# A hybrid streaming encoder step: state-space preparation and first matrices moved into the first pass, bias copies into the state-space loop

## The chip, the cores and the metric

The kernel runs on one core of a Trainium2 chip. The metric is the device time of one execution in microseconds (us), the median of several runs. Engines are named as in the profile: PE (matrix engine), with PEld for its weight loads, DVE (vector), ACT (scalar), POOL (GpSimd) and SP (the queue that issues most DMAs).

## What is computed

One layer of a hybrid encoder, for 2048 prompt frames and 8 x 16 frames of running streams (17 tiles of 128 rows):

```python
h = _rms_norm(x, norm_gain)
z = jnp.einsum('bld,de->ble', h, w_in)
u, g_s, q, k, v, g_a = jnp.split(z, SPLITS, axis=-1)
y_s, hr, hi = _s5_branch(u, a_re, ..., h0_re, h0_im)
q = _rms_norm(heads(q), q_gain)
k = _rms_norm(heads(k), k_gain)
y_a = _band_attention(q, k, v, rel_table)
mixed = jnp.concatenate([y_s * jax.nn.silu(g_s), y_a * jax.nn.silu(g_a)], axis=-1)
y = x + jnp.einsum('ble,ed->bld', mixed, w_out)
```

`_s5_branch` is a state-space model: 32 groups of 16 channels, each driving a 64-dimensional complex diagonal state that is scanned along the frames, then a GELU and a GLU. The attention of the prompt sees its own 64-frame chunk and the 8 before it, with a learned bias over clipped distance; the running streams (`_cached_attention`) see 512 cached frames.

## The kernel before

**Foreground.** Each f32 product is three matmuls of split operands (`mm3`, L189 to L191: `whi`/`wlo` by `hhi`/`hlo`). One `mm3` is a *step* here; there are 1224. `inproj` makes three passes over the 17 tiles, with two groups of 512 columns each: `u` and `k`, then `v` and `q`, then `ga` and `gs`. A tile is 16 steps, a pass 272. Then come `glu` (8 steps a tile) and `outproj` (16). Weights arrive through five `wraw` buffers; `conv_w` splits a chunk (ACT `whi` L155, DVE `wlo` L156) and lets the next one load into the freed buffer. For the next pass 16 chunks are converted during the last tile of a pass (`due`). Things to be done some steps later are put off with `defer`: a `k` or `q` tile is scaled and squared on ACT, summed on DVE (`s` L279), raised to a power on POOL (L280, L281) two steps after its end, scaled on DVE (`zs` L284) at 8 steps, and transposed on PE (`pt` L294) at 14.

**Background.** A generator runs beside it: bias rows, S5, decode (the running streams), attention. It yields the cost of what it has emitted; each foreground step gives it a credit of 650 times a share, and when the credit is used up, the foreground goes on. So all engines' orders are fixed when the program is built. The share is `R_PREP` until the flag `u` is set (two steps after the first pass), `R_S5` until S5 has ended (flag `y`), `R_DEC` until decode has ended; in the attention it is computed so that it ends with step 1148. While weights are being converted the share is 0. A generator that yields `None` waits for a flag and gives its credit back.

**S5** (L449 to L949): first the preparation on DVE (exponentials, angles, powers, `X`, `Xs`, `AH0`); then it waits for `u`, since its later pool of tiles fits into memory only when the pool of the token tiles (`xt`) has been closed. After that come `build_a` to `build_e` (the matrices of a batch of 4 groups: DVE `CA`, `VBp`; PE `pv` and `pk`; ACT `VB`, `kr`; eight small DMAs into `T`), `tables` (rotation tables, six POOL operations a group), `load_u`, `perm_u` and `step_a` (U from memory, P on ACT, `ut` on PE, UT on ACT), and a loop over 8 batches with 6 slots each.

```python
        while not self.flags.get("u"):
            yield None
```

**Bias copies:** `bias_rows` (L955) writes the bias line and then 8 copies of it, each repeated 128 times, from POOL's queue to `tl_d` in DRAM (L965). Decode and attention read them.

Of the kernel before, what the change touches and what calls it, by code (L numbers as in the profile page):

```python
# [7 lines left out]
F32 = mybir.dt.float32  # L8
# [10 lines left out]
NG, CH, NS = 32, 16, 64  # L19
# [20 lines left out]
def ap_of(t, offset, pat):  # L40
    return bass.AP(tensor=t.tensor, offset=t.offset + offset, ap=pat)


class Build:
# [148 lines left out]
    def inproj(self):  # L193
        nc, I, tc = self.nc, self.I, self.tc
        wp, hp, ev = self.wp, self.hp, self.ev
        xst = ExitStack()
        xp = self.pool(xst, "xt")
        x3 = I["x"].rearrange("(t p) d -> t p d", p=128)
        passes, W = self.PASSES, self.W

# [1 line left out]
        XR = {}  # L202

        def load_tok(t):
            xt = xp.tile([128, 1024], F32, tag="xtok", name="xtok")
            nc.sync.dma_start(xt, x3[t])
            return xt

# [179 lines left out]
        for ps in range(3):  # L388
            for ti, t in enumerate(TILES):
                if ps == 0 and ti < 2:  # L390
                    continue
                last = ti == NT - 1
                if last:
                    self.due(self.step + 4, 1.25, 16 if ps < 2 else 8)
                for gi in range(2):
                    g = passes[ps][gi]
                    z = self.psm.tile([128, 512], F32, tag="mm", name="z")
                    for k in range(8):
                        self.busy = bool(self.cq)
                        self.mm3(z, hs[0][:, k], hs[1][:, k], W[ps, gi, k], k == 0, k == 7)  # L400
                        if gi == 0 and k == 1:
                            if ps == 2 and last:
                                while not self.flags.get("y"):
                                    yield 500
                                self.glu_load(TILES[0])
                            else:
                                nxt = conv_h(ps * NT + ti + 1)
                        self.tick()
                        if ps == 2 and last and gi == 1 and k == 3:
                            self.glu_tr(TILES[0])  # L410
                            self.glu_load(TILES[1])
                        yield 650
                    EV[g](g, t, z)
                hs = nxt
            if ps == 0:
                xst.close()
            if ps == 0:
                self.defer(2, lambda: self.flags.update(u=True))

# [29 lines left out]
    def s5(self):  # L449
# [188 lines left out]
        yield 500  # L638
        pst.close()

        while not self.flags.get("u"):
            yield None

        mp = self.pool(st, "s5m", side="right", bufs=2)
        Tm = []
# [216 lines left out]
            nc.sync.dma_start(y4[c0:c0 + n, :, b * GB * CH:(b + 1) * GB * CH], y[0:n])  # L862

        SL = self.SL_S5
        for n in range(3):
            load_u(0, n)
        build_a(0)
        for q in range(2):
            for _ in tables(q):
                yield 2 * SL  # L870
        perm_u(0, 0)
        build_b(0)
        yield SL
        for n in range(3):
            if n == 1:
                build_d(0)
            feed(n)
            if n == 0:
                build_c(0)
            if n == 2:  # L880
                build_e(0)
            yield SL
        for b in range(NBATCH):
            nx = b + 1 < NBATCH
            for sl in range(6):
                if 2 <= sl:
                    step_gs(b, sl - 2)
                if sl < 4:
                    step_b1(b, sl)
                    step_swap(b, sl)  # L890
                if 1 <= sl < 5:
                    step_rot(b, sl - 1)
                if b and 1 <= sl < 4:
                    step_y(b - 1, sl - 1)
                yield SL
                if 2 <= sl:
                    step_h(b, sl - 2)
                if sl == 5:
                    step_fin(b)
                q = b * GB + sl  # L900
                tg = tables(q + 2) if sl < 4 and q + 2 < NG else iter(())
                next(tg, None)
                if b and sl < 3:
                    step_c(b - 1, sl)
                if nx:
                    if sl == 0:
                        build_a(b + 1)
                    if sl == 3:
                        build_b(b + 1)
                        yield SL  # L910
                    if sl == 4:
                        build_c(b + 1)
                        yield SL
                        build_d(b + 1)
                        yield SL
                    if sl >= 3:
                        feed(3 * (b + 1) + sl - 3)
                    if sl == 5:
                        build_e(b + 1)
                yield SL  # L920
                for _ in tg:
                    pass
# [32 lines left out]
    def bias_rows(self):  # L955
# [5 lines left out]
        nc.gpsimd.dma_start(self.rl_d, rl)  # L961
        self.st_line.close()
        yield 600
        for h in range(NH):
            nc.gpsimd.dma_start(self.tl_d[h], ap_of(self.rl_d, 768 * h, [[0, 128], [1, 767]]))  # L965
            yield 1000


    def decode(self):
# [507 lines left out]
                    self.use_spare()  # L1477


    R_PREP, R_S5, R_DEC = 0.2, 0.48, 0.75  # L1480
    MARGIN = 0
    att_left = 136
    C_PREP = 400
# [123 lines left out]
```

## Time and profile before

| what | value |
|---|---|
| median of 3 runs | 1227.88 us (1225.18 to 1228.61) |
| the profiled execution | 1226.13 us |
| its span (first to last instruction) | 1224.3 us |
| PE busy | 1193.0 us (97%) |
| DVE / ACT / POOL busy | 742.6 / 597.7 / 366.6 us |
| granted PE clock, mean | 0.995 of 2.4 GHz |
| read / written | 169.48 / 67.80 MB |

The profile is of one execution. Busy time of PE is counted from modelled ends of pipelined matmuls, so a stretch with PE fully busy is one in which it never stood still. A wait is the idle time of an engine just before an instruction, with what ended it behind the arrow. The first pass runs from the start to about 205 us, the second to about 460, the third to about 704; S5's loop fills 250 to 575 us, decode 600 to 670, attention 705 to 1160.

### The profile page before, as it was taken

The page shows a single profiled execution, that of the slowest core. Times are in us where ns is not written, and L with a number is a line of the kernel's source. Part 1 is how long each engine was busy: PE and PEld are TensorE (multiplying, and loading weights), DVE is VectorE, ACT ScalarE, POOL GpSimd, SP SyncE. Part 2 cuts the span into 40 slices and gives each one's busy share as a digit, 9 for nine tenths or more (in the row PEclk, how much of TensorE's full clock was granted, in tenths as well). Part 3 has the DMA queues.
Part 4 walks back from the last instruction along what each step waited for, and adds up shares of the span by engine and source line. Part 5 has one row for each costly group of instructions (what it writes and reads, how often), then busy time and mean ns, then how long its engine had stood idle before and what let it go on. Part 6 is the DMA issues. An engine that isn't in the chain of part 4 may idle for free.

```text
span 1224.3 us, 18936 instructions
## 1 busy us (share of the span) xinstructions
PE 1193.0 (97%) x6687; PEld 983.1 (80%) x6687; DVE 742.6 (61%) x1391; ACT 597.7 (49%) x1159; POOL 366.6 (30%) x455
## 2 busy tenths in 40 slices
PE   8999999899999998999999999999999999999998
PEld 5788888777788876887777878788888888888876
DVE  5324556868999988985444456565565555555511
ACT  6434446266666656553232346565654555455410
POOL 2433242557767735540000011111211121121120
PEclk9999999999999998999999999999999999999999
DMA  8876556655545567433895688897877777767243
GB/s 252 262 250 181 155 177 202 195 142 129 149 123 151 135 195 214 110 93 88 270 382 171 204 247 245 255 265 205 217 221 215 206 240 241 196 205 225 73 136 107
DMA packets 190119, 236.58 MB, mean 193 GB/s; under 512 B 58136, under 2 KB 122656, under 8 KB 189000
## 3 DMA queue, kind: packets, MB, share of 16 engines
q1 hardware_dynamic: 189016, 232.15, 64.2%
q0 software_dynamic: 864, 3.21, 0.8%
q8 instruction: 53, 0.87, 0.3%
q14 instruction: 42, 0.34, 0.1%
q10 hardware_dynamic: 144, 0.00, 0.0%
HBM read 169.48 MB, written 67.80 MB: 194 GB/s over the span
## 4 chain that ended last, share of the span: by engine, by line
PE 78%; DMA 6%; DVE 6%; POOL 3%; ACT 3%; issue 2%; SPq 1%; DVEq 0%; ACTq 0%; POOLq 0%
PE z L189 19%; PE z L191 18%; PE z L190 18%; PE o L1218 6%; PE pt L1200 5%; PE s L1170 5%; DMA wraw<-in_w_in_dram 3%; PE pt L294 1%; PE o L1057 1%; PE y L843 1%; SPq L701 1%; PE y L842 1%; PE v L771 1%; ACT whi L155 1%; PE s L1015 1%
## 5 line engine op out<-in xcount | busy, mean ns | idle before, releaser
L189 PE MATMUL z<-whi,hhi 128*128 128x512 f32 x816 | 339.2, 416 | 1.4 <-ACT whi L155 0.7
L190 PE MATMUL z<-wlo,hhi 128*128 128x512 f32 x816 | 321.3, 394 | 3.3 <-DVE wlo L156 3.1
L191 PE MATMUL z<-whi,hlo 128*128 128x512 f32 x816 | 320.7, 393 | 0.5 <-DVE hlo L231 0.5
L189 PEld LDWEIGHTS z<-whi,hhi 128*128 128x128 f32 x816 | 154.1, 189 | 38.9 <-issue 5.1
L190 PEld LDWEIGHTS z<-wlo,hhi 128*128 128x128 f32 x816 | 154.5, 189 | 36.5 <-DVE wlo L156 8.0
L191 PEld LDWEIGHTS z<-whi,hlo 128*128 128x128 f32 x816 | 154.0, 189 | 34.3 <-DVE hlo L231 1.0
L1207 ACT ACTIVATE pth<-pt 128x640 fp32r<-128x640 f32 (+4 forms) x128 | 81.7, 639 | 129.3 <-PE pt L1200 89.4
L1208 DVE TENSOR_TENSOR ptl<-pt,pth 128x640 fp32r<-128x640 f32 (+4 forms) x128 | 94.6, 739 | 60.6 <-ACT pth L1207 59.7
L189 PE MATMUL z<-whi,mh 128*128 128x512 f32 x272 | 113.7, 418 | 0.0
L1115 POOL MEMSET bias<- 64x64 f32 x32 | 4.7, 146 | 363.5 <-DMA bias<-tl_d 250.0
L1189 ACT ACTIVATE sn<-sn,mn 128x640 f32<-128x640 f32 (+4 forms) x128 | 96.9, 757 | 29.5 <-DVE mn L1180 29.4
L191 PE MATMUL z<-whi,ml 128*128 128x512 f32 x272 | 107.1, 394 | 1.3 <-POOL ml L1415 1.3
L190 PE MATMUL z<-wlo,mh 128*128 128x512 f32 x272 | 106.7, 392 | 0.0
L1180 DVE CUSTOM_DVE_ANT_0 sn<-s,bias 128x640 f32<-128x640 f32 (+4 forms) x128 | 93.3, 729 | 11.4 <-PE s L1170 10.4
L1170 PE MATMUL s<-ks,q 128*128 128x320 f32 (+1 forms) x448 | 87.4, 311 | 0.0
L1200 PE MATMUL pt<-ident,sn 128*128 128x128 f32 x560 | 83.0, 274 | 3.9 <-DVE ptl L1208 3.1
L1170 PEld LDWEIGHTS s<-ks,q 128*128 128x128 f32 x448 | 74.7, 188 | 11.1 <-DVE mn L1180 1.2
L1200 PEld LDWEIGHTS pt<-ident,sn 128*128 128x128 f32 x560 | 64.9, 140 | 22.5 <-ACT sn L1189 10.0
L231 DVE TENSOR_TENSOR hlo<-xraw,hhi 128x1024 fp32r<-128x1024 f32 x49 | 60.9, 1242 | 20.7 <-ACT hhi L228 20.6
L280 POOL TENSOR_SCALAR s<-s 128x8 f32<-128x8 f32 x34 | 15.9, 468 | 182.9 <-DVE s L279 182.3
L1228 DVE TENSOR_TENSOR ot<-o,tmp 64x512 f32<-64x512 f32 x32 | 22.0, 689 | 74.5 <-ACT tmp L1226 74.5
L191 PEld LDWEIGHTS z<-whi,ml 128*128 128x128 f32 x272 | 51.0, 188 | 13.2 <-POOL ml L1415 1.7
(268 smaller groups left out, 2171.3 us busy)
## 6 DMA issues: line engine op xcount, KB each, us to landing
xraw<-in_xT_dram SPq DMA_DIRECT2D x49, 512.0 KB, 4.5
q<-qt_d SPq DMA_DIRECT2D x64, 256.0 KB, 8.6
ks<-kt_d SPq DMA_DIRECT2D x28, 512.0 KB, 5.6
vhl<-vp_d SPq DMA_DIRECT2D x28, 512.0 KB, 6.7
wraw<-in_w_in_dram SPq DMA_DIRECT2D x48, 256.0 KB, 4.5
bias<-tl_d SPq DMA_DIRECT2D x32, 320.0 KB, 6.3
mt<-mt_d SPq DMA_DIRECT2D x17, 512.0 KB, 7.4
x<-in_x_dram SPq DMA_DIRECT2D x34, 256.0 KB, 5.8
```

The costliest lines, as they stand in the source:

```text
L189: mm(z, a, whi, start=first, stop=False)
L190: mm(z, a, wlo, start=False, stop=False)
L191: mm(z, b, whi, start=False, stop=last)
L231: nc.vector.tensor_sub(lo, raw, fv(hi))
L1170: nc.tensor.matmul(ps_s[:, bank, 0:wp], Q[n, x2][:, s, 128 * a:128 * a + 128], KS[n][:, s, c0:c0 + wp], start=(x2 == 0), stop=(x2 == 1))
L1180: nc.vector.tensor_tensor_reduce(out=o, in0=i0, in1=i1, scale=1.0, scalar=3e38, op0=OP.add, op1=OP.min, accum_out=mn)
L1189: nc.scalar.activation(out=sn[:, 0:w], in_=sn[:, 0:w], func=AF.Exp, scale=-1.0, bias=mn, accum_out=SUM[n][:, a, s:s + 1])
L1200: nc.tensor.transpose(t[:, k], pr[:, 128 * k:128 * k + 128], self.ident)
L1207: nc.scalar.activation(out=h, in_=t[:, 0:w], func=AF.Copy)
L1208: post.append(lambda: nc.vector.tensor_tensor(out=l, in0=t[:, 0:w], in1=fv(h), op=OP.subtract))
L1218: nc.tensor.matmul(o[:, a0:a1], VB[n][:, j, s, :], t[:, 3 * a0 + j + a0:4 * (a1 - 1) + j + 1:4], start=(y == 0 and j == 4), stop=(y == 1 a ...
L1228: post.append(lambda: nc.vector.tensor_tensor(out=ot[mine], in0=o[mine], in1=tmp[mine], op=OP.add))
```

## The change

1. The pool `xt` is gone; the token tile lives in the slot `vhl`, which is free in the first pass.
2. The wait for `u` moves behind the preparation, `build_a` to `build_e` of batch 0, the tables of the first four groups and `build_a(1)`. So these stand in the first pass; only `load_u`, `perm_u` and `step_a` come behind the wait. Later tables start with group 4.
3. The eight bias copies move from `bias_rows` into the S5 loop, one a batch.
4. `R_PREP` goes from 0.2 to 0.27, `R_S5` from 0.48 to 0.42.

```diff
@@ inproj
-        xst = ExitStack()
-        xp = self.pool(xst, "xt")
...
-            xt = xp.tile([128, 1024], F32, tag="xtok", name="xtok")
+            xt = ev.tile([128, 1024], F32, tag="vhl", name="xtok", bufs=1)
...
-            if ps == 0:
-                xst.close()
@@ s5
         pst.close()
-        while not self.flags.get("u"):
-            yield None
...
         SL = self.SL_S5
+
+        build_a(0)
+        yield SL
+        for q in range(4):
+            for _ in tables(q):
+                yield SL
+        build_b(0)
+        yield SL
+        build_c(0)
+        yield SL
+        build_d(0)
+        yield SL
+        build_e(0)
+        yield 2 * SL
+        build_a(1)
+        while not self.flags.get("u"):
+            yield None
         for n in range(3):
             load_u(0, n)
-        build_a(0)
-        for q in range(2):
-            for _ in tables(q):
-                yield 2 * SL
+        yield 2 * SL
         perm_u(0, 0)
-        build_b(0)
         yield SL
         for n in range(3):
-            if n == 1:
-                build_d(0)
             feed(n)
-            if n == 0:
-                build_c(0)
-            if n == 2:
-                build_e(0)
             yield SL
         for b in range(NBATCH):
             nx = b + 1 < NBATCH
+            self.bias_copies(b)
...
-                tg = tables(q + 2) if sl < 4 and q + 2 < NG else iter(())
+                tg = tables(q + 2) if sl < 4 and 4 <= q + 2 < NG else iter(())
...
-                    if sl == 0:
+                    if sl == 0 and b:
                         build_a(b + 1)
@@ bias_rows
-        for h in range(NH):
-            nc.gpsimd.dma_start(self.tl_d[h], ap_of(self.rl_d, 768 * h, [[0, 128], [1, 767]]))
-            yield 1000
+
+    def bias_copies(self, h):
+        self.nc.gpsimd.dma_start(self.tl_d[h], ap_of(self.rl_d, 768 * h, [[0, 128], [1, 767]]))
@@ shares
-    R_PREP, R_S5, R_DEC = 0.2, 0.48, 0.75
+    R_PREP, R_S5, R_DEC = 0.27, 0.42, 0.75
```

Counted in the built orders by foreground steps: the preparation on DVE stands at steps 56 to 178 instead of 134 to 305; the first matmul of the loop (`v`) at 297 instead of 330; from one batch to the next are 44 steps instead of 38; the last `y` matmul of S5 at 676 instead of 664; decode's first product at 724 instead of 709, attention's at 832 instead of 820, its last at 1146 instead of 1145. The bias copies stand some 45 steps apart, the last near step 610; decode reads them at 701.

The order on PE, where the first batch's U enters the S5 work (`ut` transposes it, `pk` is the matrix of batch 0, both write one PSUM buffer). Before:

```order
L733 MATMUL ut<-ident,P 128x128 x4
L686 MATMUL pk<-CA,X 16x128 x4
L189 MATMUL z<-whi,hhi 128x512
L190 MATMUL z<-wlo,hhi 128x512
L191 MATMUL z<-whi,hlo 128x512
```

In the change (lines of the new file), with the foreground's `pt` of the last `k` tile of the first pass ahead of it:

```order
L292 MATMUL pt<-ident,zs 128x128 x4
L189 MATMUL z<-whi,hhi 128x512
L190 MATMUL z<-wlo,hhi 128x512
L191 MATMUL z<-whi,hlo 128x512
L189 MATMUL z<-whi,hhi 128x512
L190 MATMUL z<-wlo,hhi 128x512
L191 MATMUL z<-whi,hlo 128x512
L727 MATMUL ut<-ident,P 128x128 x4
```

`pk` of batch 0 no longer stands behind `ut`: it is now in the first pass, five steps behind `pv`. And `ut` stands 34 steps earlier, two steps behind the `pt` of the hand-over.

The order on ACT at that place, from the last weight conversions of the second pass. Before:

```order
L155 ACTIVATE whi<-wraw,gain 128x512 x5
L303 ACTIVATE kt<-pt,kg_88 128x4x128
L274 ACTIVATE sq<-z,rstd 128x512
L275 ACTIVATE zs<-z,rstd 128x512
L228 ACTIVATE hhi<-xraw 128x1024
```

In the change:

```order
L155 ACTIVATE whi<-wraw,gain 128x512 x5
L713 ACTIVATE P<-U 128x512
L301 ACTIVATE kt<-pt,kg_88 128x4x128
L713 ACTIVATE P<-U 128x512
L728 ACTIVATE UT<-ut 128x4x128
L272 ACTIVATE sq<-z,rstd 128x512
L273 ACTIVATE zs<-z,rstd 128x512
L226 ACTIVATE hhi<-xraw 128x1024
```

Two copies of U and one of `ut` now stand ahead of the foreground's `sq`, `zs` and `hhi`. On SP the first three U loads have moved likewise, from behind the next tile's `xraw` to between the fourth and the fifth of the last weight loads.

The order on POOL where the tables begin. Before, behind the wait for `u`:

```order
L648 MEMSET T_2120 128x512
L648 MEMSET T_2122 128x512
L756 TENSOR_TENSOR cos<-cb 128x256
L757 TENSOR_TENSOR ttmp<-sb 128x256
L758 TENSOR_TENSOR cos<-cos,ttmp 128x256
L761 TENSOR_TENSOR sin<-sb,cb 128x256
L762 TENSOR_TENSOR ttmp<-cb,sb 128x256
L763 TENSOR_TENSOR sin<-sin,ttmp 128x256
L280 TENSOR_SCALAR s_2176<-s_2176 128x8
L281 TENSOR_TENSOR s_2176<-s_2176,nhalf 128x8
```

In the change, at the same place of the foreground:

```order
L278 TENSOR_SCALAR s_2167<-s_2167 128x8
L279 TENSOR_TENSOR s_2167<-s_2167,nhalf 128x8
L968 DMA tl_d<-rl_d 128x767
L278 TENSOR_SCALAR s_2287<-s_2287 128x8
L279 TENSOR_TENSOR s_2287<-s_2287,nhalf 128x8
L750 TENSOR_TENSOR cos<-cb 128x256
L751 TENSOR_TENSOR ttmp<-sb 128x256
L752 TENSOR_TENSOR cos<-cos,ttmp 128x256
```

The memsets and the first four tables are gone from here; they stand in the first pass now, nine table operations in a row ahead of an `s` there. A bias copy has come in between two `s`.

## Rows read from the trace of the kernel before

**Rows 1.** The page, part 1: busy time, share of the span, instructions.

```profile
PE 1193.0 (97%) x6687; PEld 983.1 (80%) x6687; DVE 742.6 (61%) x1391; ACT 597.7 (49%) x1159; POOL 366.6 (30%) x455
```

**Rows 2.** Stretches: start:end length, busy by engine (instructions), PE clock, DMA share, GB/s.

```profile
36.00:200.00 164.00, 164.00 (x753) 135.60 (x753) 74.17 (x140) 73.94 (x111) 62.35 (x89) 1.00 0.65 195
200.00:225.00 25.00, 22.58 (x96) 17.99 (x95) 20.84 (x39) 14.20 (x21) 6.45 (x5) 0.93 0.84 282
225.00:320.00 95.00, 90.12 (x469) 72.03 (x468) 78.19 (x126) 51.17 (x108) 66.17 (x76) 1.00 0.51 137
320.00:445.00 125.00, 125.00 (x703) 101.94 (x702) 113.32 (x195) 77.58 (x175) 85.05 (x95) 1.00 0.55 144
445.00:485.00 40.00, 35.68 (x169) 27.42 (x169) 34.43 (x53) 24.95 (x46) 16.32 (x17) 0.91 0.73 217
...
705.00:860.00 155.00, 149.65 (x876) 127.07 (x876) 91.11 (x208) 89.61 (x204) 25.48 (x44) 1.00 0.83 245
```

**Rows 3.** PE's waits, 225 to 320 us: total us, times, longest.

```profile
PE pk L686 <- ACT UT L734: 2.0, 1, 2.0
PE pt L294 <- DVE zs L284: 1.5, 2, 1.0
PE ut L733 <- ACT VB L679: 1.3, 1, 1.3
```

**Rows 4.** PE's waits, 445 to 485 us.

```profile
PE pt L294 <- DVE zs L284: 2.8, 2, 2.4
```

**Rows 5.** PE in order of time: start, length, and in brackets the idle time before.

```profile
250.51 0.41 PE L686 MATMUL pk<-CA,X 128*16 128x128 f32 x8 [1.96 <-ACT UT L734]
```

**Rows 6.** POOL and PE in order of time, 232 to 245 us.

```profile
232.94 0.99 POOL L648 MEMSET T<- 128x512 f32 x2 [5.76 <-DVE AH0s L637]
...
239.21 1.77 POOL L763 TENSOR_TENSOR sin<-sin,ttmp 128x256 f32<-128x256 f32 x1
...
244.27 0.63 PE L294 MATMUL pt<-ident,zs 128*128 128x128 f32 x4 [1.02 <-DVE zs L284]
```

**Rows 7.** ACT, DVE and PE in order of time, 443 to 473 us.

```profile
446.39 2.55 ACT L155 ACTIVATE whi<-wraw,gain 128x512 fp32r<-128x512 f32 x4
...
457.16 2.79 ACT L155 ACTIVATE whi<-wraw,gain 128x512 fp32r<-128x512 f32 x4 [6.24 <-DMA wraw<-in_w_in_dram]
...
443.75 0.76 DVE L661 TENSOR_TENSOR CA<-CA,btmp 128x576 f32<-128x576 f32 x1
...
450.57 2.73 DVE L156 SCALAR_TENSOR_TENSOR wlo<-wraw,gain,whi 128x512 fp32r<-128x512 f32 x4
...
472.84 1.09 PE L294 MATMUL pt<-ident,zs 128*128 128x128 f32 x4 [2.35 <-DVE zs L284]
```

**Rows 8.** U and P: duration ns min/median/max, first and last start; landing of U's DMAs.

```profile
L711 SPq DMA_DIRECT2D U<-u_d x24: 538/590/1111, 232.9 to 496.7; - x24
L719 ACT ACTIVATE P<-U x24: 610/626/647, 245.6 to 523.8; 128x512 f32<-128x512 f32 x16, 16x512 f32<-16x512 f32 x8
...
DMA to landing us min/median/max: 3.3/4.1/5.2
```

**Rows 9.** SP's queue and PE in order of time at the first hand-over.

```profile
215.60 2.74 SPq L139 DMA_DIRECT2D wraw<-in_w_in_dram  x5
...
221.35 0.63 PE L191 MATMUL z<-whi,hlo 128*128 128x512 f32 x1
```

**Rows 10.** A stretch of that hand-over (columns as in rows 2).

```profile
218.00:220.00 2.00, 1.27 (x6) 1.18 (x7) 2.00 (x4) 0.49 (x1) 1.28 (x1) 0.79 1.03 383
```

**Rows 11.** POOL's groups, 225 to 560 us: busy us, mean ns of one, idle before.

```profile
L763 POOL TENSOR_TENSOR sin<-sin,ttmp 128x256 f32<-128x256 f32 x32 | 30.5, 953 | 2.5
...
L756 POOL TENSOR_TENSOR cos<-cb 128x256 f32<-128x256 f32 x32 | 24.1, 753 | 24.6 <-DVE t L809 24.6
```

**Rows 12.** The bias copies on POOL: issue in ns, first and last start; landing.

```profile
L965 POOL DMA_DIRECT2D tl_d<-rl_d x8: 523/626/662, 37.6 to 73.6; - x8
...
DMA to landing us min/median/max: 4.9/7.1/8.2
```

## Prediction, made before the changed kernel ran

> **What bounds the kernel now.** I read the page's busy times first: PE works 1193.0 of 1224.3 us [rows 1], so a change that adds and removes no matmul can only win or lose in the 31 us in which PE is idle and in the time it runs at its lower clock. The stretches say where that is [rows 2]: between 36 and 200 us PE is never idle, nor between 320 and 445; it is idle 95.00 - 90.12 = 4.9 us from 225 to 320, where the state-space (S5) work begins, and 40.00 - 35.68 = 4.3 us from 445 to 485, where the second pass hands over to the third. There the granted clock is 0.91 too: 0.09 x 40 = 3.6 us lost at the lower of the two levels (1.2 instead of 2.4 GHz), which it took after PE had stood still. DVE is then the busiest engine behind PE: 113.32 of 125.00 us from 320 to 445.
>
> PE's waits name the causes. From 225 to 320 [rows 3]: 2.0 us `pk` for ACT's `UT` copy, 1.5 us `pt` for DVE's `zs`, 1.3 us `ut` for ACT's `VB` copy. From 445 to 485 [rows 4]: 2.8 us `pt` for `zs`, 4.3 - 2.8 = 1.5 us in other waits. The reader should see that no wait of the first group is for data from far away: each is a short PE step that stands right behind another one whose result an engine in between has not yet copied, or (`zs`) a small POOL operation behind the rotation tables.
>
> **Part A, the start of the S5 work (225 to 320 us): -3.9 us.** The 2.0 us wait is one event: `pk` stands directly behind `ut` on PE, both use the one `ut` buffer, and PE waits 1.96 us until ACT has copied it [rows 5]. In the change that `pk` (batch 0) stands in the first pass with five foreground steps ahead of it, about 5 x 0.7 us, so all 2.0 us go. (A step is 0.7 us: 164 us [rows 2] hold 753 matmuls, 52 to a tile of 16 steps, so 0.71.) Of the `zs` wait 1.0 us is the tables: POOL clears two T tiles from 232.94, works on one table until 240.98, and only then comes to `s`; PE gets its `pt` at 244.27 after 1.02 us [rows 6]. The change puts these tables ahead of the wait for `u`; 1.0 us goes. What is left of the group, 1.9 us, is the ordinary traffic of the first batches, now spread over 44 steps a batch instead of 38; I let half of it go, 0.9. Sum 3.9; bounds 2.0 (the one event alone) and 4.9 (all).
>
> **Part B, second pass to third (445 to 485 us): -2.5 us.** ACT makes the first `whi` at 446.39 to about 447.1, but DVE, which has run without a gap through build_a and a rotation, makes the first `wlo` at 450.57 [rows 7]: 3.4 us of DVE queue. The next five weight chunks are only loaded when `wlo` frees their buffers, and ACT waits 6.24 us for them [rows 7]; the chain goes round three times and ends in `zs` and PE's longest wait, 2.35 us to 472.84 [rows 7]. The share R_S5 falls by 0.42/0.48 = 0.875, so DVE's share of 0.91 must fall to between 0.91 x 0.875 = 0.79 (all of it background) and 0.91 (none of it). I take half of the queue away, 1.7 us, and with it 0.8 of the 3.6 us of clock. Bounds: 0 (the loads set the chain whatever DVE does) and 4.3 + 3.6 = 7.9.
>
> **Part C, the new wait at the first hand-over (216 to 226 us): +1.0 us.** The first U loads move from 232.9 us [rows 8] to the moment `u` is set: on SP they now stand inside the last five weight loads, on ACT the first `P` copy stands ahead of `kt`, `sq` and `zs`, on PE the first `ut` stands two steps behind `pt`. Four of the five loads issued from 215.60 in 2.74 us [rows 9] bring the first U to 217.8; landing takes 3.3 to 5.2, median 4.1 [rows 8], and `P` 0.63: 222.5 us. PE would stand there after the matmul that starts at 221.35 [rows 9], 0.43 later: a wait of 0.7 us (0 to 1.8). I take 1.0, because the DMA engines are full at that time (1.03, 383 GB/s [rows 10]). ACT is late by some 3 us behind `P`; its `sq` and `zs` free a PSUM buffer that PE next needs eight steps later, over 5 us, so that costs nothing. Bound above: rival 2.
>
> **Part D, what is moved into the first pass: 0.** DVE's preparation moves from steps 134 to 305 to steps 56 to 178, between evictions. From 36 to 200 us DVE has 74.17 of 164 us, POOL 62.35 [rows 2], and PE does not wait; what now runs after about 218 us and before POOL is let go at 232.94 [rows 6], 15 us at most, and one more build_a (six operations like the one of 0.76 us in [rows 7]) come in: 20 us of DVE. POOL gets four tables of six operations, 0.75 to 0.95 us each [rows 11]: about 20 us. Bunched, it is tight: three operations (2.6 us) every 800/(0.27 x 650) = 4.6 steps or 3.2 us are 0.81 of POOL, and its present work is 0.38; for 37 steps (26 us) it falls behind by 0.19 x 26 = 5 us. The cover is that `s` is asked for two steps after a tile's end and `pt` stands at fourteen, 8.5 us later. If the tables took that cover, it would cost what the wait behind a table costs now, 1.0 us [rows 6], in each of the two tiles. The xtok tile in the `vhl` slot costs nothing: `v` writes there only in the second pass. The wait for `u` holds only generators back, no engine.
>
> **Part E, the bias copies: 0.** Eight issues of 0.63 us on POOL, 4.9 to 8.2 us to land [rows 12], go from 37.6 to 73.6 us into the S5 loop, one a batch. PE does not wait where they leave [rows 2]; POOL has 85.05 of 125 us where they come, plus about 2. Behind each stand the next `s` and table operations, 0.6 us later. The last is issued some 90 steps before decode reads it.
>
> **Part F, the later end: 0.** S5 ends 12 steps later, so attention starts at step 832 instead of 820 and is packed into 315 instead of 327 steps, 4% denser. PE's idle time in its first part, 155.00 - 149.65 = 5.4 us from 705 to 860 [rows 2], would grow by 0.2; at 25% growth 1.3 is the bound.
>
> **The sum:** -3.9 - 2.5 + 1.0 = -5.4 us. The profiled execution took 1226.1 us (span 1224.3), so it would be 1220.7; the median of the runs lies 1.8 above it, 1227.9, so I forecast 1222.5.
>
> **Rivals.** *1: the loads alone set the second hand-over.* Then B is 0 and the sum -2.9: 1225.0. For it: ACT's 6.24 us wait is for a DMA; against it: the loads start when `wlo` frees the buffers, and `wlo` was late.
>
> *2: the U wait takes the place of what A removes (slower).* One transfer in the wrong place: U's 256-byte pieces behind five weight loads. Priced by the slowest landing for a transfer of this kernel on a busy queue, 8.2 us [rows 12]: U at 226.0, `P` 226.6, a wait of 4.8 us instead of 1.0 right after the wait that already lowered the clock; the lower level held for one more such stretch (0.07 x 25 = 1.75 us lost from 200 to 225 [rows 2]) makes it 6.6. With A at its lower bound and B at 0: +4.6, 1232.5. It decides from the point where the U landing takes about 7 us. For it: PE, ACT and SP all carry the chain at one place; against it: no landing of U shown is over 5.2 us [rows 8].
>
> *3: the copies' issue blocks POOL.* The row shows 0.52 to 0.66 us an issue in the first pass [rows 12], where DVE is 0.45 busy; none is shown beside a DVE at 0.91. If each held POOL until a `zs` comes as late as the one behind the tables, 1.02 us of PE [rows 6], eight cost 8.2: 1230.7. Against it: `s` stands a table's length away from most copies. The Trainium skill, SBUF — State Buffer (SBUF: two separate sides), speaks against the change here: a DMA issued from GpSimd needs a port that DVE's two-port operations lock, and one that takes about 620 ns alone took about 3100 beside a copy. By its figure, an estimate, eight issues would hold POOL 8 x 2.5 = 20 us more; it also says that only copies and the like lock it so, and DVE in this loop runs two-input operations, so I give it little.
>
> *4: more goes than I let go:* A at 4.9 and B at 5: 1219.0. That the change doesn't do what it says (preparation not done when `u` is set) is excluded by the order: build_a(1), the last piece, stands on DVE ahead of the conversion of the second pass's weights.
>
> **Chances.** The forecast 0.50 (its own range 1219 to 1225), rival 1 0.22, rival 2 0.13, rival 3 0.07, rival 4 0.08. A measurement of this kernel can tell about 0.3%, 3.7 us, from no change: below 1224.2 is faster, above 1231.6 slower. Forecast and rival 4 give 0.54 faster (0.04 of the forecast lies within), rival 1 and half of rival 3 make 0.30 the same, rival 2 and the other half 0.16 slower. The range, 1217.0 to 1230.0, leaves out rival 2, half of rival 3 and the extreme of B.
>
> **What would show it.** Right: no `pk` wait for `UT` and no `pt` wait behind a table between 225 and 320 us; the first `wlo` of the second hand-over less than 2 us behind its `whi`; PE idle there under 3 us. C is right if PE's first `ut` waits for `P` by 0 to 1.8 us. Wrong: a `ut` wait of several us with the clock at 1.2 GHz behind it (rival 2); the second hand-over unchanged with DVE idle before `wlo` (rival 1); POOL issues of over 2 us (rival 3); PE idle between 36 and 200 us (D). If all four show as forecast and the time still doesn't fall, the loss must lie in the denser attention.

## The result: slower by 0.9%, with the profile after

| what | before | changed |
|---|---|---|
| median | 1228.25 us (6 runs) | 1236.91 us (6 runs, 1235.08 to 1244.26) |
| ratio of the runs | | 1.0087, 95% interval 1.0066 to 1.0107 |
| the profiled execution | 1226.13 us | 1235.08 us |
| its span | 1224.3 us | 1233.3 us |

Forecast were 1222.5 us and a range up to 1230.0. PE's work is the same (first line, against [rows 1]), so again only its idle time and its clock can differ. The page's busy times of the changed kernel:

```profile
PE 1194.2 (97%) x6687; PEld 983.8 (80%) x6687; DVE 735.7 (60%) x1391; ACT 598.9 (49%) x1159; POOL 365.4 (30%) x455
```

The stretches of the changed kernel, columns as in [rows 2]:

```profile
200.00:225.00 25.00, 22.36 (x101) 17.84 (x99) 18.62 (x24) 15.30 (x23) 7.57 (x6) 0.99 0.83 258
225.00:320.00 95.00, 92.20 (x477) 74.68 (x476) 67.19 (x119) 56.55 (x118) 49.65 (x56) 0.97 0.59 162
320.00:445.00 125.00, 124.78 (x694) 101.41 (x693) 111.23 (x183) 73.25 (x162) 86.43 (x98) 1.00 0.56 151
445.00:485.00 40.00, 35.96 (x188) 28.42 (x187) 33.49 (x49) 28.11 (x54) 16.74 (x18) 1.00 0.72 225
...
705.00:860.00 155.00, 144.68 (x823) 121.77 (x821) 83.40 (x197) 83.76 (x193) 26.86 (x45) 0.98 0.85 244
860.00:1140.00 280.00, 275.98 (x1621) 239.60 (x1620) 159.72 (x305) 146.76 (x271) 45.67 (x59) 1.00 0.72 215
```

From 225 to 320 us PE is idle 2.8 instead of 4.9 us, but at a granted clock of 0.97 instead of 1.00, which takes 0.03 x 95 = 2.9 us (from 200 to 225 us it is the other way round, 0.99 instead of 0.93). So little is won there, but the main loss is not where the change was made. The GLU's first product says so: up to it PE has the same 3811 instructions in both kernels, and the changed one is 1.3 us ahead (changed, then before):

```profile
703.77 0.39 PE L189 MATMUL z<-whi,yh 128*128 128x512 f32 x1
```

```profile
705.05 0.39 PE L189 MATMUL z<-whi,yh 128*128 128x512 f32 x1
```

From there to the end of PE's work it takes 525.4 us, the kernel before 514.4, with the same 2876 instructions. The loss stands from 705 us on: 10.3 instead of 5.4 us idle up to 860, where the clock falls too, and 4.0 us from 860 to 1140, where the kernel before has this row (1.4 us):

```profile
860.00:1140.00 280.00, 278.63 (x1636) 243.21 (x1634) 160.66 (x306) 147.57 (x272) 49.90 (x62) 1.00 0.74 213
```

PE's waits in the changed kernel: the only one left from 225 to 320 us, those at the second hand-over (445 to 485), at the GLU's start (700 to 745) and behind 860 us (total us, times, longest):

```profile
PE ut L727 <- ACT P L713: 2.8, 1, 2.8
...
PE v L765 <- DVE t L785: 3.1, 1, 3.1
PE ut L727 <- ACT VB L673: 1.0, 1, 1.0
...
PE ty L1346 <- DMA y<-y_d: 6.1, 2, 4.8
PE tm L1361 <- POOL ms L1402: 0.4, 1, 0.4
...
PE pt L1202 <- ACT sn L1191: 2.6, 4, 0.7
PE o L1220 <- ACT pth L1209: 1.5, 1, 1.5
```

The `pk` wait and the `zs` wait behind a table [rows 3] are gone. New are the wait of the first U, and 6.1 us for the GLU's input `y` (before: 1.4). SP's queue there tells why; in order of time, start, length, issue, first of the changed kernel:

```profile
701.27 0.42 SPq L1338 DMA_DIRECT2D y<-y_d  x1
701.80 1.56 SPq L139 DMA_DIRECT2D wraw<-in_w_out_dram  x3
703.40 1.14 SPq L1136 DMA_DIRECT2D q<-qt_d  x2
704.59 0.58 SPq L1375 DMA_DIRECT2D gs<-gs_d  x1
705.22 1.62 SPq L1136 DMA_DIRECT2D q<-qt_d  x2
707.56 0.33 SPq L1338 DMA_DIRECT2D y<-y_d  x1
...
717.41 0.72 PE L1346 MATMUL ty<-ident,y 128*128 128x128 f32 x4 [4.84 <-DMA y<-y_d]
```

And of the kernel before:

```profile
703.06 1.57 SPq L139 DMA_DIRECT2D wraw<-in_w_out_dram  x3
704.68 0.42 SPq L1114 DMA_DIRECT2D bias<-tl_d  x1
705.16 0.42 SPq L1373 DMA_DIRECT2D gs<-gs_d  x1
708.46 0.32 SPq L1336 DMA_DIRECT2D y<-y_d  x1
```

In the kernel before, the attention's first `ks`, `q` and `vhl` loads were issued between steps 781 and 797, ahead of the conversion of the GLU's weights (steps 801 to 814), in which the share is 0. In the changed kernel they come some sixteen steps later: `ks` just goes ahead of the conversion, and the four `q` loads come behind it, between the GLU's `y` loads. The `y` issued at 707.56 us is there 9.85 us later (717.41); PE stands 4.84 us, and its granted clock falls. The same 17 us, changed, then before:

```profile
703.00:720.00 17.00, 10.94 (x48) 8.56 (x47) 4.12 (x6) 2.49 (x4) 1.26 (x1) 0.88 1.01 255
```

```profile
703.00:720.00 17.00, 15.54 (x81) 12.41 (x80) 8.44 (x21) 7.51 (x19) 1.57 (x3) 1.00 0.92 269
```

### The profile page after: what moved, and what is told of

Same layout as the page of the kernel before. It is cut to its first block, busy times and chain, and to the rows that moved or that the text cites. A ratio compares the mean times of both kernels' runs of the same rounds, so it can differ in the third digit from the quotient of the medians.

```text
span 1233.3 us, 18904 instructions
## 1 busy us (share of the span) xinstructions
PE 1194.2 (97%) x6687; PEld 983.8 (80%) x6687; DVE 735.7 (60%) x1391; ACT 598.9 (49%) x1159; POOL 365.4 (30%) x455
## 4 chain that ended last, share of the span: by engine, by line
PE 81%; DMA 8%; DVE 4%; ACT 3%; SPq 2%; issue 2%; POOL 0%; DVEq 0%; ACTq 0%; POOLq 0%
PE z L189 19%; PE z L191 19%; PE z L190 19%; PE o L1220 6%; PE pt L1202 5%; PE s L1172 5%; DMA wraw<-in_w_in_dram 3%; PE pt L292 1%; PE y L837 1%; PE v L765 1%; PE y L836 1%; PE o L1059 1%; PE ut L727 1%; DMA y<-y_d 1%; DMA bias<-tl_d 1%
## 5 line engine op out<-in xcount | busy, mean ns | idle before, releaser
L1172 PE MATMUL s<-ks,q 128*128 128x320 f32 (+1 forms) x448 | 87.5, 311 | 0.0
L1202 PEld LDWEIGHTS pt<-ident,sn 128*128 128x128 f32 x560 | 64.9, 140 | 26.0 <-ACT sn L1191 13.7
L278 POOL TENSOR_SCALAR s<-s 128x8 f32<-128x8 f32 x34 | 15.2, 447 | 184.3 <-DVE s L277 183.9
L1402 POOL TENSOR_TENSOR ms<-ms,gs 128x512 f32<-128x512 f32 x16 | 20.6, 1287 | 158.6 <-DMA gs<-gs_d 118.2
```

The costliest lines, as they stand in the source:

```text
L1172: nc.tensor.matmul(ps_s[:, bank, 0:wp], Q[n, x2][:, s, 128 * a:128 * a + 128], KS[n][:, s, c0:c0 + wp], start=(x2 == 0), stop=(x2 == 1))
L1202: nc.tensor.transpose(t[:, k], pr[:, 128 * k:128 * k + 128], self.ident)
```

## The experiments

**A common measure.** Kernels whose steps stand at other times are compared by foreground steps. The table gives, for each pair of neighbouring PE instructions, the time from start to start less the median for that kind of pair over all 17 profiles, summed by steps; it counts waits and time at the lower clock alike. Only differences between rows mean something: in steps 884 to 1156 PE of the kernel before stands idle 2.9 us, and the table has 21.9.

```
steps             0-68 68-272 272-340 340-544 544-578 578-646 646-816 816-884 884-1156 1156- total
before             8.7   1.5     7.3    14.8     9.1     3.8    17.2    10.8     21.9    1.6  96.7
e2_old_late        7.3   1.5     8.4    14.4     6.8     3.9    17.2    15.9     28.3    0.0 103.5
e8_old_later      11.1   1.5     8.5    14.3     6.5     3.9    17.2     9.8     33.7    5.3 111.8
e9_old_vhl         7.4   1.5     9.3    14.2     7.7     3.8    17.2    10.6     22.3    0.0  94.0
e10_old_copies    11.7   1.5     7.3    16.2     7.6     3.8    17.2    11.3     22.2    1.8 100.6
changed           10.8   1.8    10.4    11.1     6.0     3.7    18.4    14.3     30.8    0.0 107.2
e1_s5_048         12.8   1.8    12.5    13.8     4.9     3.6    21.2     6.5     20.9    0.0  97.9
e3_u_later        13.0   1.8     6.6    10.6    10.0     3.1    19.1    14.9     26.1    1.7 106.9
e4_dec_088        11.6   1.8    10.3    11.1     5.5     3.7    20.2     8.6     23.3    0.1  96.0
e5_line_late      15.3   2.3    11.3    11.1     7.2     3.7    18.3    11.6     30.4    0.0 111.1
e6_all_048        11.0   2.3    14.5    14.2    11.2     3.3    18.4     7.2     21.4    0.0 103.4
e7_all_045        12.3   2.3    13.7    13.0     4.7     4.3    16.5    10.5     22.6    0.0  99.9
e11_u8_046        12.9   1.8     6.7    14.8     8.3     3.4    17.9    13.8     21.6    0.8 102.0
e12_u8_048         9.1   1.8     8.4    15.2    10.1     3.4    21.4     9.0     26.3    0.0 104.7
e13_loads_first   10.9   1.8     9.9    11.1     6.1     3.7    19.5     8.3     30.0    0.0 101.2
e14_pass_u6       13.3   1.8     6.5    10.5     8.9     5.7    19.0     8.7     22.8    0.2  97.5
e15_pass_u2       10.9   1.8    10.0    11.1     5.9     4.4    17.5     8.0     22.8    0.4  92.8
```

The first five have one order of work up to step 781 (but for a slot or the copies), and show how far executions of one order differ: 7.3 to 11.7 in the first column, 6.5 to 9.1 at the second hand-over.

A second measure needs no medians: the time from the GLU's first product to the end of PE's work. PE has the same 2876 instructions there in every kernel whose attention starts behind that product:

| kernel | us | | kernel | us |
|---|---|---|---|---|
| before | 514.4 | | changed | 525.4 |
| e9_old_vhl | 512.9 | | e5_line_late | 522.2 |
| e10_old_copies | 515.3 | | e3_u_later | 523.1 |
| e2_old_late | 524.4 | | e13_loads_first | 518.5 |
| e8_old_later | 529.4 | | e4_dec_088 | 511.8 |
| e11_u8_046 | 516.4 | | e15_pass_u2 | 511.3 |
| e14_pass_u6 | 511.9 | | | |

Each run was timed beside the kernel before, whose median lay between 1226.1 and 1228.3 us. So a difference between the medians of two experiments is good to about 2 us only, and the ratios are the safer figures.

### The attention's place

**e2_old_late**, the kernel before, with

```diff
         yield from self.decode()
+        yield 7000
         self.flags["dec"] = True
```

> The kernel before, with a yield of 7000 ahead of the attention and nothing else: its first loads move from step 781 to 797 and its first product from 820 to 832, step for step where the changed kernel has them. Theory F: slower by 8 to 14 us than before, 1236 to 1242, with a wait of PE for the GLU's y of 4 to 6 us at about step 816. Rival L: within 4 us of before, 1224 to 1232.

Measured: 1238.62 us, ratio 1.0103 (1.0067 to 1.0139). The old kernel, with nothing but its attention put where the changed one has it, loses all that the change lost. Its profiled execution (1233.04 us) is one of its fastest, yet it takes 10.0 us more than the kernel before behind the GLU's first product (second measure). Its rows show the same two places, `y` at the GLU's start (700 to 745 us) and ACT's `sn` behind 860 us (before: no wait for `sn` there):

```profile
PE ty L1344 <- DMA y<-y_d: 3.3, 1, 3.3
...
PE pt L1200 <- ACT sn L1189: 4.0, 5, 1.7
```

**e4_dec_088**, the reverse in the changed kernel:

```diff
-    R_PREP, R_S5, R_DEC = 0.27, 0.42, 0.75
+    R_PREP, R_S5, R_DEC = 0.27, 0.42, 0.88
```

> The changed kernel with R_DEC at 0.88 instead of 0.75: S5 as changed, the decode denser, the attention's first loads at step 781 and its first product at 821, as before the change. Theory F: the time falls by 7 to 12 us, to 1225 to 1230; PE's wait for the GLU's y under 2 us. Rival L: no change, 1234 to 1238, or slower by the denser decode.

Measured: 1226.93 us (1.0001; 0.9979 to 1.0023), 10.0 below the changed kernel (by the ratios 10.6). Steps 816 to 1156 fall from 45.1 to 31.9 us; the denser decode takes 1.8 back. So the loss hangs on the attention's place in both directions.

**e1_s5_048**, the changed kernel with the old share:

```diff
-    R_PREP, R_S5, R_DEC = 0.27, 0.42, 0.75
+    R_PREP, R_S5, R_DEC = 0.27, 0.48, 0.75
```

> The changed kernel with R_S5 at 0.48 again (all else as changed). S5's last matmul moves from step 676 to 629, the attention's first loads from step 797 to 749, its first product from 832 to 776. Theory F (the loss lies in the attention's later start: its first loads stand ahead of the GLU's first loads on SP, and it is packed denser): PE's wait for the GLU's first y, 6.1 us in the changed kernel, falls under 2 us, and the attention's stretch gets its idle time of before back; with the second hand-over back at DVE 0.91 (up to 3 us of its gain lost) 1218 to 1226 us. Rival L (the loss lies in the preparation and the loop, that is the U wait and a loop that is too slow or too fast): 1233 us or more, since the U wait (2.8 us) stays and the second hand-over is worse.

Measured: 1225.23 us (0.9991; 0.9973 to 1.0008). Two things were not expected: the second hand-over isn't worse with the old share (4.9 us), and the loop (340 to 544) loses 2.7 of the 3.7 us that the changed kernel has gained there.

**e8_old_later**, as e2, with more:

```diff
         yield from self.decode()
+        yield 24000
```

> The kernel before, with a yield of 24000 ahead of the attention: its first loads at step 842, behind the GLU's start, its first product at 860, 40 steps later than before. If the loss of the 12 steps is mostly the loads standing ahead of the GLU's y, that wait is back to 1.4 us or less and the time is 1230 to 1236, not slower than with 12 steps (1238.6). If it is mostly the denser attention (340 slots in 288 steps instead of 328), the pt waits for ACT's sn grow over 4.0 us and the time is over 1242.

Measured: 1240.90 us (1.0111; 1.0082 to 1.0139). Between the two theories: the `y` waits are down to 1.0 us, but steps 884 to the end have 39.0 us in the table instead of 28.3 (e2). So a later attention costs time also where its first loads are out of the way.

**e13_loads_first** takes the loads out of the way and leaves the attention late and dense:

```diff
         for f in loads(0):
             f()
-            yield 3 * SL
         for n in range(2):
             bias(n)
-            yield 3 * SL
+        yield 24 * SL
```

> The changed kernel with the attention's first eight loads issued without yields between them (steps 793 to 807, ahead of the conversion of the GLU's weights) and the same sum of yields behind them: its first product stays at step 832, as changed. If the loss at the GLU's start is these loads ahead of the GLU's y on SP and on the DMA engines: the two waits of PE for y, 6.1 us, fall under 2 us, the idle time of steps 816 to 884 from 14.3 to about 10.5 us, and what is left, the denser attention, keeps its 28 to 31 us of idle time in steps 884 to 1156: 1230 to 1234. If the loads are all of the loss: 1226 to 1229. If they have no part: 1237.

Measured: 1232.86 us (1.0048; 1.0033 to 1.0063): 4.0 us below the changed kernel. The stretch that lost 4.6 us of PE:

```profile
703.00:720.00 17.00, 15.87 (x82) 12.83 (x81) 7.67 (x14) 6.07 (x12) 2.00 (x2) 1.00 0.59 189
```

One `y` wait of 1.3 us is left, and steps 884 to 1156 keep 30.0 us. So the place of the loads is one part of the loss: 4.0 us by the medians, 6.9 of 11.0 us by the two profiles (second measure). The rest goes with the later attention itself; which part is the larger the runs leave open.

### The wait for U

**e3_u_later**, the changed kernel with the first perm_u put off (and `R_DEC` 0.84, which keeps the attention's place):

```diff
             load_u(0, n)
-        yield 2 * SL
+        yield 6 * SL
         perm_u(0, 0)
```

> The changed kernel with 6 instead of 2 slots between load_u and the first perm_u, and R_DEC at 0.84 so that the attention starts where it does in the changed kernel (first loads at step 797, first product at 833). Theory C (the 2.8 us ut wait and the lower clock behind it are one event, U's landing): the wait goes and the time falls by 2.8 to 5 us, 1232 to 1234. Rival: the wait only moves to the next thing that needs U or P: time unchanged, 1237.

Measured: 1233.70 us (1.0050; 1.0024 to 1.0076), 3.2 below the changed kernel, but the two intervals overlap, and the totals of the table are 106.9 and 107.2: a gain isn't shown. The `ut` wait is gone, and steps 272 to 340 fall from 10.4 to 6.6 us, but 4 us come back at the second hand-over. The loop is twelve steps later there, so other S5 steps stand beside the hand-over; that this is the reason was not tried by itself.

**e6_all_048** has three edits in the changed kernel (the second is that of the next section):

```diff
-        yield 2 * SL
+        yield 4 * SL
         perm_u(0, 0)
...
         self.st_line.close()
-        yield 600
+        yield 4000
...
-    R_PREP, R_S5, R_DEC = 0.27, 0.42, 0.75
+    R_PREP, R_S5, R_DEC = 0.28, 0.48, 0.75
```

> The changed kernel with three things mended at once: the yield of 4000 behind the bias line, 4 instead of 2 slots between load_u and perm_u, R_S5 0.48 (R_PREP 0.28). Theory (gains and losses add): against the run with R_S5 0.48 alone, 1225.2 us, the start gives 3 to 5 us and the ut wait 3 to 5: 1216 to 1220. Rival (what is taken away comes back at the second hand-over, as it did with 6 slots): 1222 to 1226.

Measured: 1231.35 us (1.0035; 1.0018 to 1.0051), a miss, and worse than e1. The second hand-over took 11.2 us, and with 4 slots the U wait only moved on, to the first `v`, which needs `UT` (220 to 260 us):

```profile
PE v L765 <- ACT UT L728: 3.6, 1, 3.6
```

**e7_all_045**, the same with `R_S5` 0.45 in the last line:

> The same with R_S5 0.45: the attention's first loads at step 777 and its first product at 816, where the kernel before has them (781 and 820). Theory (gains and losses add): against the run with R_DEC 0.88, 1226.9 us, 3 us from the start and 3 to 4 from the ut wait: 1219 to 1222. Rival as above: 1223 to 1227.

Measured: 1227.21 us (1.0005; 0.9986 to 1.0025), the rival's number: 13.7 us at the first hand-over, again with the `v` wait.

**e11_u8_046**, the changed kernel with 8 slots:

```diff
-        yield 2 * SL
+        yield 8 * SL
         perm_u(0, 0)
...
-    R_PREP, R_S5, R_DEC = 0.27, 0.42, 0.75
+    R_PREP, R_S5, R_DEC = 0.27, 0.46, 0.75
```

> The changed kernel with 8 instead of 2 slots between load_u and perm_u and R_S5 0.46, so that the attention's first loads are at step 781 and its first product at 818 (before: 781 and 820). Neither the U wait nor the attention's place can cost then. If these two are all that ate the gain, the loop's gain is left over: 1220 to 1224. If the loop's gain comes from the low share alone and the start is slower, 1225 to 1229.

Measured: 1225.38 us (0.9976; 0.9953 to 0.9998). No U wait (6.7 us in steps 272 to 340), but no gain in the loop either (14.8), and the time is in the second of the two ranges.

**e12_u8_048**, the same with `R_S5` 0.48:

> The same with R_S5 0.48: the attention's first loads at step 765, its first product at 790. Against the run with R_S5 0.48 and 2 slots (1225.2 us) the U wait and the lower clock behind it go, 4 to 5 us: 1219 to 1222. If the wait only moves into the loop, as with 4 slots: 1225 or more.

Measured: 1230.05 us (1.0020; 0.9998 to 1.0041), a miss: the U wait is gone, the second hand-over has 10.1 us, and the attention, though it starts at step 790, 26.3. So an earlier attention wasn't a cheaper one in this profile.

### The start, the copies and the slot

In the profiles of the changed order and its variants PE reaches step 102 at 87.5 to 91.5 us (one: 85.8), in the kernel before at 84.8. The first idea was a wait of DVE that the removed copies had hidden: `sgp`, the first tile of S5, lies in the memory of the bias line, so DVE waits for the line's DMA (20 to 40 us, changed kernel):

```profile
DVE sgp L455 <- DMA rl_d<-rl: 6.5, 1, 6.5
```

**e5_line_late** puts the S5 preparation 13 steps later:

```diff
         self.st_line.close()
-        yield 600
+        yield 4000
...
-    R_PREP, R_S5, R_DEC = 0.27, 0.42, 0.75
+    R_PREP, R_S5, R_DEC = 0.28, 0.42, 0.75
```

> The changed kernel with a yield of 4000 instead of 600 behind the bias line (R_PREP 0.28 instead of 0.27, so that from the first U load on every step is the changed kernel's). DVE's first write of the S5 preparation, the memset of sgp, goes from step 25 to 38 and stands behind the landing of the line (rl_d). Theory G (sgp reuses the line's memory, DVE stands 6.5 to 7.8 us until the line has landed, and ACT's hhi, DVE's hlo and the evictions of the first tile stand behind it): the 6.5 us wait goes, PE reaches step 68 at 60 to 61 us instead of 63.7 to 66.1, and the time falls by 2 to 5 us, to 1232 to 1235. Rival (the late hhi is a late landing of xraw, the order of DVE has no part): unchanged, 1237, and step 68 still at 63 us or later.

Measured: 1239.41 us (1.0099; 1.0073 to 1.0125). The theory fell: the `sgp` wait is gone, and `hhi` is as late as ever, now plainly for its `xraw` (24 to 46 us):

```profile
ACT hhi L226 <- DMA xraw<-in_xT_dram: 9.4, 2, 6.9
```

**e9_old_vhl**, the kernel before with part 1 of the change alone (the pool `xt` goes as well):

```diff
-            xt = xp.tile([128, 1024], F32, tag="xtok", name="xtok")
+            xt = ev.tile([128, 1024], F32, tag="vhl", name="xtok", bufs=1)
```

> The kernel before with part 1 of the change alone: the token tile in the slot vhl, no pool xt; every instruction at its old step. If the slot is why the first tile's xraw lands late in the profiles of all changed kernels (issue to hhi 5.5 to 8.6 us, before 4.8 to 5.4): PE at step 102 at 88 to 91 us instead of 84 to 88, time 1228 to 1231. If not: 1226, within 2 us of before.

Measured: 1226.19 us (0.9993; 0.9974 to 1.0011). The slot shows no cost.

**e10_old_copies**, the kernel before with part 3 alone:

```diff
         for h in range(NH):
-            nc.gpsimd.dma_start(self.tl_d[h], ap_of(self.rl_d, 768 * h, [[0, 128], [1, 767]]))
             yield 1000
...
             nx = b + 1 < NBATCH
+            self.bias_copies(b)
```

> The kernel before with part 3 alone: the eight bias copies in the S5 loop, one a batch, their old places left as empty yields, so that all else stands at its old step. Part E of the prediction (nothing): 1226, within 2 us of before, no issue on POOL over 1 us that PE waits behind. Rival 3 of the prediction (the issues hold POOL until a zs comes late): 1230 or more, with PE waits for zs in the loop.

Measured: 1227.33 us (1.0001; 0.9980 to 1.0022). The copies show no cost (at most 2.7 us within the interval). Yet this profile is at 11.7 us in steps 0 to 68, with all that stands ahead of that `xraw` as in the kernel before, and e8, too, has 11.1. So the old order, too, can be as late. The mean of the nine profiles with the changed order up to there is 11.7 us (9.1 to 13.3), that of the five old ones 9.2 (7.3 to 11.7): some 2 us may well belong to the change, but what would make them was not found.

### The share, pass by pass

In the table steps 340 to 544 have 10.5 to 11.1 us in each profile with a share of 0.42, and 13.0 to 16.2 in all others. So the low share made that gain, not the moved preparation (the low share in the old order was not tried), and the low share is also what made S5 end later. **e15_pass_u2** takes it only where it pays:

```diff
         if not self.flags.get("y"):
-            return self.R_S5
+            return self.R_S5 if self.step < 578 else 0.5
```

> The changed kernel with R_S5 0.42 up to step 578 and 0.50 behind it, 2 slots as changed: first loads at step 778, first product at 817; decode at its old share. Against the changed kernel (1236.9 us) only the attention's place is given back, 10 to 12 us: 1224 to 1227, with the U wait of 2 to 3 us still there. If the place of the attention is worth less: 1228 or more.

Measured: 1222.84 us, ratio 0.9959 (0.9943 to 0.9974): 14.1 below the changed kernel, a little better than expected. It is the only version below the 1224.2 us from which the prediction would call it faster; e11's interval, too, ends just under 1. Its stretches (GLU's start, attention):

```profile
705.00:745.00 40.00, 38.86 (x223) 33.07 (x223) 23.44 (x62) 23.45 (x62) 5.74 (x10) 1.00 0.89 264
860.00:1140.00 280.00, 277.85 (x1625) 242.93 (x1625) 161.02 (x305) 146.61 (x271) 48.08 (x60) 1.00 0.72 214
```

**e14_pass_u6**, the same with 0.54, and 6 slots for U:

```diff
-        yield 2 * SL
+        yield 6 * SL
         perm_u(0, 0)
...
-            return self.R_S5
+            return self.R_S5 if self.step < 578 else 0.54
```

> The changed kernel with 6 slots between load_u and perm_u, and R_S5 0.42 up to step 578 (the end of the second hand-over), 0.54 behind it: the attention's first loads at step 781, its first product at 818. The idle time of steps 340 to 544 is 11 us in every profile with 0.42 and 13 to 15 with 0.45 to 0.48 or in the kernel before. If that gain of 3 to 4 us is the share's, and is kept once the U wait and the attention's place cost nothing: 1220 to 1224. If the second hand-over takes it back (10.0 us there with 6 slots, 6.0 in the changed kernel): 1225 to 1228.

Measured: 1225.72 us (0.9998; 0.9977 to 1.0020), the second of the two ranges: the first hand-over is 3.5 us better than in e15, the second 3.0 worse, and S5 at 0.54 costs 1.3 more in steps 578 to 646.

## Why the prediction was wrong

**The step that failed is part F**, "the later end: 0", bound 1.3. The shift of twelve steps was known, and was priced by the mean density of the attention alone. It measured 12.5 us in the old kernel (e2) and 10.0 and 14.1 us when it was undone in the changed one (e4, e15). Behind the GLU's first product, where PE's work is the same, the profiles say 11.0 us for the change and 10.0 for e2. Two things were missed. First, a transfer's place: the attention's loads are issued some 40 steps ahead of its first product, and a stretch with the share 0 lies between; where they fall behind it, they stand ahead of loads for which PE waits (4.0 us by the medians, e13). Second, twelve steps of place aren't priced by an idle share: they cost 6 to 9 us in steps 884 to 1156. PE's idle time there rises from 2.9 to 9.1 us in the changed kernel, in single waits: `sn` 2.8 us in five (before 0.7 in two), `ptl` 2.4 in four (1.1 in two), and one each for `pth` (1.5), `ms` (1.4) and `mo` (1.0). Whether the smaller room makes them, or which steps now fall beside which tile, stays open, since each run moves both. Room alone doesn't explain them: the table has 20.9 to 23.3 us in ten profiles with the first product between steps 776 and 821, without a trend, 26.3 in one at 790, and 26.1 to 30.8 at 832 and 833. The last sentence of the prediction named the denser attention as the place of a loss that the four other parts didn't show; no rival and no chance stood for it.

**Part A** (-3.9) was right in its two events, the `pk` wait and the table's, which are gone; steps 290 to 340, where they stood, lose some 2 us less than in the five old profiles. The ordinary traffic, which had 0.9 us, was mis-sized: it gave 3.7 (14.8 as the mean of the five old profiles, 11.1 now) in the longer stretch 340 to 544, and by the share: with 0.46 or 0.48 the table has 13.8 to 15.2 again.

**Part C** (+1.0, bound 1.8) was mis-sized. The first U was issued at 221.83 us and `P` began at 227.63, so U took up to 5.8 us, where 4.1 was reckoned; SP's queue, later by 4 us, and PE's arrival moved together. PE waited 2.8 us (1.9 to 3.7 in other runs of this order), and the clock behind it was 0.97 up to 320 us. In the four plain profiles of this order (changed, e4, e13, e15) steps 272 to 340 have 10.2 us, in the old ones 8.2: the new wait took 2 us more than A's two events gave back there, so it cost some 4 us where 1.0 was forecast. Rival 2's mechanism is there, with a wait of 2.8 us instead of the 4.8 that it reckoned with; it did not need a landing of 7 us.

```profile
221.83 4.31 SPq L705 DMA_DIRECT2D U<-u_d  x3
...
227.63 0.63 ACT L713 ACTIVATE P<-U 128x512 f32<-128x512 f32 x1 [6.09 <-DMA U<-u_d]
...
228.32 0.90 PE L727 MATMUL ut<-ident,P 128*128 128x128 f32 x3 [2.79 <-ACT P L713]
```

**Part B** (-2.5): the first `wlo` now starts 1.3 us behind its `whi`, as forecast (before 4.2), and the clock stays at 1.00. But PE's idle time there is 4.0 us, not under 3: other waits, `v` and `ut`, took the place. By steps it is 5.9 against a mean of 7.5 in the old profiles, -1.6, and the profile on which B was built (9.1) was the worst of the five. The reason given, the lower share, doesn't hold: 4.9 us with 0.48, 10.0 with 0.42 and a loop twelve steps later. That it counts which S5 steps meet the hand-over would fit these numbers; it was not tried by itself.

**Part D** (0): from step 68 to 272 the table has 1.8 instead of 1.5 us. The sign that was to show it wrong, PE idle between 36 and 200 us, is there: 1.9 us instead of none, all ahead of 66 us. But e10, with the old order, has 1.7 us there, so the moved work is not shown to be the cause; the first 68 steps stay open, as above. **Part E** (0): right as far as e10 can tell, and with it rival 3 with its 8.2 us is out. The issues in the loop:

```profile
L968 POOL DMA_DIRECT2D tl_d<-rl_d x8: 561/617/665, 233.3 to 523.2; - x8
```

Beside a DVE at 0.89 of the stretch they are as long as in the first pass [rows 12]. The 3100 ns of the Trainium skill (SBUF — State Buffer, section SBUF: two separate sides, under A bandwidth-pool intuition that's wrong) do not show here; it gives them for a DMA beside a copy on DVE.

**The sum.** What was argued for A, B and C as -5.4 measures 2.0 - 3.7 - 1.6 = -3.3 us up to step 578 (A's two events and C stand together in the 2.0), and the start may take 2 of them. The time itself says the same: from step 68 to the GLU's first product, with the same work on PE, the five old profiles take 641.2 to 643.8 us (mean 642.7), the changed kernel, e13 and e15 638.6 to 640.1 (mean 639.3). With the attention in its place and the low share where it pays, e15 gets -4.6 by the medians; there 2.9 us of it lie in steps 816 to 884, where its loads come three steps earlier than in the kernel before. The direction was right for what the change does up to there, and wrong for the time, since the later end cost 10 us and more.

## What to carry to other kernels

When a change makes a background stage end later, follow the first transfers of the next stage, not its first product: list them in their queue, and see what they pass on the way, above all a stretch in which the background stands still. Don't price a later, more tightly packed stage by its mean idle share; move it alone in the old kernel by the same number of steps and measure (here one line). And compare several profiles of the old kernel before a term is built on one stretch: the second hand-over differed by 2.6 us between executions of one order.

## What was not expected of the hardware

- A transfer of 256 KB that is there in 5.4 us or less (e13: `y` issued at 707.39, used at 712.75) takes 9.85 us when four `q` loads were issued in the 4.2 us before it. The DMA share is 1.01 in those 17 us against 0.59 in e13. The Trainium skill (DMA: Bandwidth & Descriptors, section Queues, rings and completion order) says that each DMA engine takes the descriptors of a ring in order; the late landing fits that, but the order itself no run here shows.
- With that one wait of 4.84 us PE's granted clock was 0.88 in the 17 us around it, so at the lower of its two levels (1.2 instead of 2.4 GHz) for part of them, as at the first hand-over (0.97 over 95 us with a wait of 2.8 us).
- The `xraw` load at 28 to 30 us was used 4.7 to 8.6 us after its issue (issue to `hhi`, 17 profiles), with PE up to 3.8 us idle behind it, in one and the same place of the program.
